# Squared-ReLU MLP of a decoder step: the down projection by Strassen's seven products, in a second pass over operands kept in DRAM

## The chip, the cores and the metric

The kernel runs on one core of one Trainium2 chip. The metric is the device time of one execution in microseconds (us); a lower time is better. The engines are TensorE (PE, its weight loads PEld), VectorE (DVE), ScalarE (ACT), GpSimd (POOL) and SyncE (SP), which issues DMAs. Each engine works through its own instructions in the order in which they were emitted, and waits on semaphores for the others.

## The reference

One layer of a decoder trunk on 1024 prompt tokens and 8 new tokens (T = 1032 columns) with 1024 features. Sparse attention and a gated mixing branch make `m`; the change is in what follows:

```python
    x = x + m @ w_o                                  # 1024 x 1024
    hf = rmsnorm(x, g_ffn)
    x = x + jnp.square(jax.nn.relu(hf @ w_up)) @ w_down   # 1024 -> 4096 -> 1024
    hp = rmsnorm(x, g_ple)
    x = x + jax.nn.sigmoid(hp @ w_pg) * (p @ w_p)    # p has 256 features
```

## The kernel before

Features lie on the 128 partitions and tokens along the free dimension. Every large product is made in float32 precision out of three matmuls: operand and weight are split into a rounded high part and the rest (`hh`, `hl`; `whi`, `wlo`), and `hi*hi`, `hi*lo`, `lo*hi` are added up in PSUM. A high part is an ACT cast, the rest a DVE or POOL subtraction behind it. `dense` makes such a product in three groups of 344 tokens, each in one of four PSUM banks of tag "mm"; `weight()` loads and splits blocks of 128x1024 weights (512 KB) ahead of their use.

The MLP runs over 8 blocks `f` of 512 hidden features. In each block, four column blocks of `w_up` (72 matmuls of 344 columns each) leave PSUM through DVE: `z = p * n1.R`, where `R` is the token's norm scale along the free dimension, then relu and square in one DVE operation, then the ACT cast `hh` and the POOL subtraction `hl`. Behind them, four blocks of `w_down` are multiplied with `hh`, `hl`, and DVE adds each PSUM group onto `x1`. So both projections are 2304 matmuls of 344 columns. In the last block the second norm follows each finished `x1[k]`: `split` is an ACT activation `nh` and a DVE operation `nl`; `square` is an ACT square and a POOL addition onto `acc` (the last one on DVE). The loop on the per-layer embedding then makes, for each of 8 column blocks, 18 matmuls of `p @ w_p` (leaving through ACT as `e`) and 72 of `w_pg`.

All of these tiles come out of one pool of 37 slots of 128x1032 floats (tag "s", reused first in, first out); a `wide` tile has all 8x1032 columns, and there is one. There is no scheduler at this place: the order of the emitted Python is the order on every engine.

Of the kernel before, what the change touches and what calls it, by code (L numbers as in the profile page):

```python
# [16 lines left out]
P = 128  # L17
# [16 lines left out]
FFB = 8  # L34
EPS = 1e-6
# [13 lines left out]
class Counted:  # L49
    """An engine whose instructions' estimated times are added up as they are emitted."""  # L50
# [15 lines left out]
def step_kernel(ctx, tc, xT, pT, w_in, w_o, w_up, w_down, w_pg, w_p, gv, gqk, wsT, b_s,  # L66
# [55 lines left out]
    # ------------------------------------------------------------ order of emission  # L122
# [46 lines left out]
    # ------------------------------------------------------------ weights, two blocks ahead  # L169
    plan = [(w_in[c], KC, pool if c > 1 else dve) for c in range(w_in.shape[0])]  # L170
    plan += [(w_o[c], KC, dve) for c in range(KC)]
    for f in range(FFB):
        plan += [(w_up[4 * f + c], KC, dve) for c in range(4)]
        plan += [(w_down[f, c], 8, dve) for c in range(4)]
    for c in range(KC):
        plan += [(w_p[c], 2, dve), (w_pg[c], KC, dve)]
# [19 lines left out]
    def weight():  # L196
        n = at[0]
        at[0] += 1
        split_weight(n)
        if n + 1 != w_in.shape[0]:  # L200
            split_weight(n + 1)
        if not n + 1 <= w_in.shape[0] <= n + 2:
            load_weight(n + 2)
        if n + 1 < len(plan) and plan[n + 1][1] < KC:
            split_weight(n + 2)
            load_weight(n + 3)
# [14 lines left out]
    def dense_in_step(A, jobs, hook=None, lag=0):  # L221
        """As dense for several blocks of weights (weights, groups, PSUM), block of features by block of
        features, for operands that are still being made."""
        n = len(A[0])
        for step in range(n + lag * (len(jobs) - 1)):
            for j, ((hi, lo), groups, outs) in enumerate(jobs):
                k = step - lag * j
                if not 0 <= k < n:
                    continue
                for w, x in ((hi, A[0]), (hi, A[1]), (lo, A[0])):  # L230
                    for (a, b), p in zip(groups, outs):
                        mm(p[:, :b - a], w[:, k, :], x[k][:, a:b],
                           start=(k == 0 and w is hi and x is A[0]), stop=(k == n - 1 and w is lo))
# [33 lines left out]
    def inv_rms(sq, n, name, then, make=bank2, wait=later):  # L267
        """sq [P, T]: squares, summed over blocks of features -> [token of tile, tile] of rsqrt(mean + eps)."""
# [11 lines left out]
    def along_tokens(r, name):  # L280
        """[token of tile, tile] -> the same values along the free dimension, on every partition."""
# [10 lines left out]
    def across(out, col):  # L292
        """A column of values along the free dimension of 64 partitions."""
# [3 lines left out]
    # ------------------------------------------------------------ constants, and the input's pre-norm  # L297
# [28 lines left out]
    # work for the tensor engine until the first operands arrive  # L326
# [40 lines left out]
    # ------------------------------------------------------------ indexer keys, weights and queries  # L367
# [9 lines left out]
    def split_heads(q, a, b, p, then=None):  # L377
        """Two heads' features -> for each its high part on its own 64 partitions, the low part on the others."""
# [65 lines left out]
    # ------------------------------------------------------------ scores and their top keys  # L444
# [76 lines left out]
    # ------------------------------------------------------------ queries and keys  # L521
# [5 lines left out]
    def head_scale(sq, f, then=None):  # L527
        """sq [P = two heads, T] -> f [token of tile, tile, head] = r / sqrt(r^2 mean + eps)."""
# [82 lines left out]
    # ------------------------------------------------------------ values  # L611
# [27 lines left out]
    # ------------------------------------------------------------ decode: 8 new tokens over paged keys  # L639
# [191 lines left out]
    # ------------------------------------------------------------ the attention branch's gate  # L831
# [9 lines left out]
    # ------------------------------------------------------------ the spatial gating branch  # L841
# [124 lines left out]
    # ------------------------------------------------------------ prompt attention  # L966
# [47 lines left out]
    # the rest of the last gate's projection fills the tensor engine while the attention starts  # L1014
# [179 lines left out]
    # the new tokens' rows, then the halves that the output projection starts with  # L1194
# [26 lines left out]
    # ------------------------------------------------------------ output projection  # L1221
# [5 lines left out]

    def in_step(A, hook=None, W=None):
        return dense_in_step(A, [(W or weight(), GROUPS, [bank("acc") for _ in GROUPS])], hook)[0]
# [172 lines left out]
```

## Time and the profile before

| | us |
|---|---|
| time, median of 3 runs (lowest to highest) | 1866.78 (1866.0 to 1867.72) |
| span of the profiled execution | 1864.2 |
| PE busy in the span | 1826.8 (98%) |
| DVE, ACT, POOL busy in the span | 1105.0, 605.4, 437.0 |

The span is that of one profiled execution, from its first to its last instruction; the time of a run also holds what lies around the span, some 2.6 us. Shares of busy time are means over stages that have different limits. In the trace, a matmul's row shows when it starts and how long it is in the pipeline; since matmuls overlap, what one costs in a stream is the distance from start to start.

### The profile page before, as it was taken

To read this page: it belongs to the slowest core of one execution; us is meant where nothing else is said; L and a number is where in the kernel's file an instruction comes from. 1 tells how busy PE (TensorE), PEld (TensorE's weight loads), DVE (VectorE), ACT (ScalarE), POOL (GpSimd) and SP (SyncE) were. 2 spreads that over 40 slices of the span, in tenths; PEclk is the share of its full clock that TensorE was granted. 3 is DMA by queue.
4 is the path that set the end of the run, shared out by engine and by line. 5 is a ranking of instruction groups with operands and counts; after the bars stand their busy time and mean duration, and the time that the engine had idled before them with its cause. 6 is when DMAs were issued, how large, how long until landed. Compare 5 with 4: busy or idle time off the path is not lost.

```text
span 1864.2 us, 28776 instructions
## 1 busy us (share of the span) xinstructions
PE 1826.8 (98%) x11722; PEld 1724.2 (92%) x11722; DVE 1105.0 (59%) x2110; ACT 605.4 (32%) x1084; POOL 437.0 (23%) x375
## 2 busy tenths in 40 slices
PE   8999989999999999999999999999999999999998
PEld 8998879998999996777699999999999999999998
DVE  7489978989877856777743434333333333335433
ACT  5554332244312136777622202020202020113322
POOL 3233354456323221110011202010101011112221
PEclk9999989999999999999999999999999999999999
DMA  4122133222222264223232111111111111111121
GB/s 171 61 93 102 58 111 105 86 86 96 64 91 77 83 165 118 60 64 94 68 117 69 34 57 45 47 46 46 46 46 46 46 46 55 48 46 49 43 77 72
DMA packets 81748, 136.66 MB, mean 73 GB/s; under 512 B 9608, under 2 KB 54544, under 8 KB 81616
## 3 DMA queue, kind: packets, MB, share of 16 engines
q1 hardware_dynamic: 79424, 130.08, 21.3%
q0 software_dynamic: 2048, 4.72, 0.8%
q8 instruction: 92, 1.51, 0.3%
q14 instruction: 40, 0.33, 0.1%
q10 hardware_dynamic: 144, 0.02, 0.0%
HBM read 105.03 MB, written 29.77 MB: 72 GB/s over the span
## 4 chain that ended last, share of the span: by engine, by line
PE 83%; DVE 7%; issue 3%; POOL 3%; ACT 1%; DMA 1%; SPq 0%; POOLq 0%; DVEq 0%; ACTq 0%
PE acc L60 69%; PE po L60 4%; PE sc L60 4%; PE pp L60 4%; DVE mask L60 3%; DVE m L60 1%; POOL wlo L193 1%; DVE qs L60 1%; PE mix L60 1%; DMA kib<-cache_ki,idx 1%; POOL pg L651 0%; PE lg L60 0%; PE dix L60 0%; PE vt L60 0%; POOL x L342 0%
## 5 line engine op out<-in xcount | busy, mean ns | idle before, releaser
L60 PE MATMUL acc<-xh,whi 128*128 128x344 f32 (+1 forms) x1144 | 373.1, 329 | 2.8 <-DVE s_q L60 1.8
L60 PE MATMUL acc<-xl,whi 128*128 128x344 f32 (+1 forms) x1144 | 365.3, 323 | 2.2 <-DVE xl L60 2.2
L60 PE MATMUL acc<-xh,wlo 128*128 128x344 f32 (+1 forms) x1144 | 365.3, 323 | 1.8 <-POOL r_x L270 1.1
L60 PE MATMUL acc<-nh,whi 128*128 128x344 f32 x960 | 302.6, 320 | 0.4 <-DVE y L60 0.3
L60 PE MATMUL acc<-nh,wlo 128*128 128x344 f32 x960 | 301.5, 319 | 0.0
L60 PE MATMUL acc<-nl,whi 128*128 128x344 f32 x960 | 301.4, 319 | 0.0
L60 PE MATMUL acc<-hh,whi 128*128 128x344 f32 x768 | 245.7, 320 | 0.0
L60 PE MATMUL acc<-hl,whi 128*128 128x344 f32 x768 | 245.5, 320 | 0.0
L60 PE MATMUL acc<-hh,wlo 128*128 128x344 f32 x768 | 245.3, 319 | 0.0
L60 DVE TENSOR_TENSOR x<-acc,x 128x344 f32<-128x344 f32 x216 | 109.3, 514 | 224.6 <-PE acc L60 224.6
L60 PEld LDWEIGHTS acc<-xh,whi 128*128 128x128 f32 x1144 | 216.6, 190 | 11.5 <-issue 5.0
L1290 POOL TENSOR_TENSOR hl<-z,hh 128x344 fp32r<-128x344 f32 x96 | 90.0, 938 | 584.8 <-ACT hh L1289 563.6
L60 PEld LDWEIGHTS acc<-xl,whi 128*128 128x128 f32 x1144 | 216.4, 190 | 3.6 <-DVE xl L60 3.2
L60 PEld LDWEIGHTS acc<-xh,wlo 128*128 128x128 f32 x1144 | 216.2, 190 | 2.7 <-POOL r_x L270 1.5
L1289 ACT CAST hh<-z 128x344 fp32r<-128x344 f32 x96 | 46.1, 480 | 501.0 <-DVE z L60 501.0
L60 PEld LDWEIGHTS acc<-nh,whi 128*128 128x128 f32 x960 | 179.3, 188 | 2.1 <-issue 0.8
L60 PEld LDWEIGHTS acc<-nh,wlo 128*128 128x128 f32 x960 | 179.4, 188 | 0.0
L60 PEld LDWEIGHTS acc<-nl,whi 128*128 128x128 f32 x960 | 179.4, 188 | 0.0
L60 DVE MATCH_REPLACE8 mask<-m,mask 128x384 f32<-128x384 f32 (+2 forms) x192 | 166.6, 875 | 0.0
L192 ACT CAST whi<-wraw 128x1024 fp32r<-128x1024 f32 (+1 forms) x136 | 134.4, 1006 | 91.8 <-DMA wraw<-w_up 66.0
L60 DVE TENSOR_TENSOR wlo<-wraw,whi 128x1024 fp32r<-128x1024 f32 (+1 forms) x91 | 108.9, 1198 | 92.9 <-ACT whi L192 88.8
L60 DVE MAX8 m<-mask 128x8 f32<-128x384 f32 (+2 forms) x192 | 161.0, 879 | 0.0
(266 smaller groups left out, 2901.4 us busy)
## 6 DMA issues: line engine op xcount, KB each, us to landing
wraw<-w_in SPq DMA_DIRECT2D x48, 512.0 KB, 3.7
wraw<-w_up SPq DMA_DIRECT2D x32, 512.0 KB, 3.1
wraw<-w_down SPq DMA_DIRECT2D x32, 512.0 KB, 3.1
q_d<-qs SPq DMA_DIRECT2D x16, 512.0 KB, 3.2
qst<-q_d SPq DMA_DIRECT2D x16, 512.0 KB, 4.9
x<-xT SPq DMA_DIRECT2D x15, 516.0 KB, 8.4
sga_d<-sg SPq DMA_DIRECT2D x8, 516.0 KB, 2.9
msgu_d<-u SPq DMA_DIRECT2D x8, 516.0 KB
```

The costliest lines, as they stand in the source:

```text
L60: return fn(*args, **kw)
L192: act.copy(hi, raws[n])
L193: eng.tensor_tensor(out=lo, in0=raws[n], in1=hi.bitcast(F32), op=ALU.subtract)
L1289: act.copy(h[:, a:b], z)
L1290: pool.tensor_tensor(out=l[:, a:b], in0=z, in1=h[:, a:b].bitcast(F32), op=ALU.subtract)
```

## The change

The hidden layer is no longer used as it is made. In a first pass over all 8 blocks, the up projection's PSUM groups leave through ACT (relu) and POOL (square), without the norm scale. With the hidden features of a block cut into two halves and the tokens into two halves of 516 (`TH`), a 2x2 block matrix is there, and `operands` makes the seven right-hand operands of Strassen's scheme (Winograd's form) of it: four are differences of 516 columns on DVE; each of the seven is split into a high part (ACT cast) and a rest (DVE subtraction) in a slot `hop`. They go to a DRAM scratch `h_d`, except those of the last block, which stay in SBUF and are the first of the second pass.

The second pass has 32 steps (8 blocks `f`, the resident block first, and 4 output pairs `o`). A step loads 512 KB of `w_down`, makes four sums of 256 columns on POOL, splits three weights and four sums (ACT casts, DVE subtractions `dlo`), and runs seven products `a`, `b`, `c`, `d` of 12 matmuls of 258 columns (`TQ`) each: 2688 in all. What a product gives is added by DVE onto `acc` and `u2` in SBUF (in the first block it is copied by ACT). In the last block, `u2` is added, the result is multiplied by `R2 = R*R`, the residual `xr` is loaded again from DRAM and added (POOL, for the last pair DVE), and the second norm follows. The embedding's products are made in two halves of 72 matmuls, one between the passes (`embed(0)`) and one behind the second (`embed(1)`), and go through a DRAM scratch `e_d`.

The core of the diff (lines are left out where `...` stands):

```diff
+    h_d = drm.tile([FFB - 1, 7, 2, P, 2, TH], F32, name="h_d")
+    e_d = drm.tile([P, KC, T], F32, name="e_d")
+    hw = wide("hw")
+    own_ops = {}
+    pieces = []
...
+        def keep(i, src):
+            def piece():
+                op = slot("hop", [P, 2, TH], F32R)
+                act.copy(op[:, 0], src)
+                dve.tensor_tensor(out=op[:, 1], in0=src, in1=op[:, 0].bitcast(F32), op=ALU.subtract)
+                if f == DOWN[0]:
+                    own_ops[i, j] = op
+                else:
+                    sp.dma_start(out=h_d[f, i, :, :, j, :].rearrange("h p t -> p h t"), in_=op.bitcast(F32))
+            return piece
+        return [keep(0, b11), less(t1, b12, b11), keep(1, t1), keep(2, b21), keep(3, b22), less(t3, b22, b12),
+                keep(4, t3), less(t2, b22, t1), keep(5, t2), less(t4, b21, t2), keep(6, t4)]
+    for f in range(FFB):
+        for j in range(2):
+            row = 4 * j
+            for q, c in enumerate((j, j + 2)):
+                h = hw[:, row + q, :]
+                for a, b, p in (dense(X1) if f + j + q else in_step(X1, n1.hook)):
+                    z = part("z")
+                    act.activation(z, p, AF.Relu)
+                    pool.tensor_tensor(out=h[:, a:b], in0=z, in1=z, op=ALU.mult)
+                    for _ in range(2):
+                        if pieces:
+                            pieces.pop(0)()
+            while pieces:
+                pieces.pop(0)()
+            pieces = operands(f, j, row)
+    R2 = n1.R
+    pool.tensor_tensor(out=R2, in0=R2, in1=R2, op=ALU.mult)
...
+    def embed(g, between=None):
+        ph, pl = [], []
+        for k in range(2):
+            e = slot("pe")
+            sp.dma_start(out=e, in_=pT[k])
+            h, l = slot("ph", dt=F32R), slot("pl", dt=F32R)
+            act.copy(h, e)
+            dve.tensor_tensor(out=l, in0=e, in1=h.bitcast(F32), op=ALU.subtract)
+            ph.append(h)
+            pl.append(l)
+        raw = slot("pwraw", [P, 4, 2, P])
+        hi, lo = slot("pwhi", [P, 4, 2, P], F32R), slot("pwlo", [P, 4, 2, P], F32R)
+        sp.dma_start(out=raw, in_=w_p[4 * g:4 * g + 4].rearrange("c p k m -> p c k m"))
+        act.copy(hi, raw)
+        dve.tensor_tensor(out=lo, in0=raw, in1=hi.bitcast(F32), op=ALU.subtract)
+        def project():
+            for n in range(4):
+                e = slot("e")
+                for a, b, p in dense((ph, pl), W=(hi[:, n], lo[:, n])):
+                    act.activation(e[:, a:b], p, AF.Copy, scale=0.5)
+                sp.dma_start(out=e_d[:, 4 * g + n, :], in_=e)
+        return project
...
+    steps = [(f, o) for f in DOWN for o in range(4)]
...
+    def down_sums(n):
+        if n < len(steps):
+            w = draw[n]
+            a11, a12, a22, a21 = (w[:, q] for q in range(4))
+            ds[n] = s_ = slot("ds", [P, 4, 2, P])
+            pool.tensor_tensor(out=s_[:, 0], in0=a21, in1=a22, op=ALU.add)
+            pool.tensor_tensor(out=s_[:, 1], in0=s_[:, 0], in1=a11, op=ALU.subtract)
+            pool.tensor_tensor(out=s_[:, 2], in0=a11, in1=a21, op=ALU.subtract)
+            pool.tensor_tensor(out=s_[:, 3], in0=a12, in1=s_[:, 1], op=ALU.subtract)
...
+        def to(self, out, first):
+            views = [(out.rearrange("p (s c) -> p s c", s=2), self.all)] if self.one else \
+                [(out[:, TQ * s:TQ * s + TQ], self.at[s]) for s in range(2)]
+            for o, p in views:
+                if first:
+                    act.copy(o, p)
+                else:
+                    dve.tensor_tensor(out=o, in0=p, in1=o, op=ALU.add)
...
+    def product(n, f, i, w, pair, start):
+        hi, lo = dhalf[n, w[0]]
+        hi, lo = hi[:, w[1]], lo[:, w[1]]
+        for j in range(2):
+            xh, xl = right(f, i, j)
+            for l, x in ((hi, xh), (hi, xl), (lo, xh)):
+                for s in range(2):
+                    mm(pair.at[s], l[:, j, :], x[:, TQ * s:TQ * s + TQ],
+                       start=(start and j == 0 and l is hi and x is xh),
+                       stop=(j == 1 and l is lo), skip_group_check=not start)
...
+    first_embed = embed(0)
+    down_sums(0)
+    for part_ in range(2):
+        down_hi(0, part_)
+        down_lo(0, part_)
+    first_embed()
+    while pieces:
+        pieces.pop(0)()
+    acc = wide("acc")
+    u2s = [slot("u2", [P, 2, TH]) for _ in range(2)]
-    for f in range(FFB):
...
+    for n, (f, o) in enumerate(steps):
+        down_load(n + 2)
+        first, last = f == DOWN[0], f == DOWN[-1]
...
         if last:
-            n2 = Norm(3, "2")
...
+            xr = [slot("xr") for _ in range(2)]
+            for h in range(2):
+                sp.dma_start(out=xr[h], in_=x1_d[:, o + 4 * h, :])
...
+        a = Pair("pa", True)
+        product(n, f, 0, A11, a, True)
+        a.to(u2, first)
+        d = Pair("pd", True)
+        product(n, f, 1, S1, d, True)
+        d.to(c22, first)
+        down_sums(n + 1)
+        down_hi(n + 1, 0)
+        product(n, f, 2, A12, a, False)
+        a.to(c11, first)
+        free(2)
+        product(n, f, 3, S4, d, False)
+        d.to(d12, first)
+        free(3)
+        down_lo(n + 1, 0)
+        down_hi(n + 1, 1)
+        c = Pair("pc", False)
+        product(n, f, 4, S3, c, True)
+        c.to(c22, False)
+        free(4)
+        b = Pair("pb", False)
+        product(n, f, 5, S2, b, True)
+        b.to(u2, False)
+        free(5)
+        down_lo(n + 1, 1)
+        product(n, f, 6, A22, c, False)
+        c.to(c21, first)
+        free(6)
...
+        if last:
+            dve.tensor_tensor(out=d12, in0=d12, in1=u2, op=ALU.add)
+            both = acc[:, 2 * o + 1, :].rearrange("p (s c) -> p s c", s=2)
+            dve.tensor_tensor(out=both, in0=both, in1=u2.unsqueeze(1).to_broadcast([P, 2, TH]), op=ALU.add)
+            for h in range(2):
+                k = o + 4 * h
+                x = n2.x[k]
+                dve.tensor_tensor(out=x, in0=x, in1=R2, op=ALU.mult)
+                (pool if o < 3 else dve).tensor_tensor(out=x, in0=x, in1=xr[h], op=ALU.add)
+                n2.square(k)
+            for k in ((), (0, 4), (1, 5), ())[o]:
+                n2.split(k)
+    last_embed = embed(1)
+    load_weight(at_pg)
+    load_weight(at_pg + 1)
+    for k in (2, 6, 3, 7):
+        n2.split(k)
+    split_weight(at_pg)
+    last_embed()
...
     for k in range(KC):
         e = slot("e")
-        for a, b, p in dense((ph, pl)):
-            act.activation(e[:, a:b], p, AF.Copy, scale=0.5)
+        sp.dma_start(out=e, in_=e_d[:, k, :])
```

On PE, one block of the down projection before the change is 24 matmuls of 344 columns for each token group, of which these are the first; `acc` is the PSUM bank:

```order
L60 MATMUL acc<-hh,whi 128x344
L60 MATMUL acc<-hl,whi 128x344
L60 MATMUL acc<-hh,wlo 128x344
L60 MATMUL acc<-hh,whi 128x344
```

After the change, one product of a step is these rows; both token quarters use one weight, so that two matmuls of 258 columns stand behind each other:

```order
L63 MATMUL pa<-hop,dhi 128x258 x4
L63 MATMUL pa<-hop,dlo 128x258 x2
L63 MATMUL pa<-hop,dhi 128x258 x4
L63 MATMUL pa<-hop,dlo 128x258 x2
```

On ACT, between the two passes of the changed kernel stand these rows (`ph`, `pwhi` belong to the embedding, `e` is its result, `hop` are operands of the resident block, `u_13652` is `u2`):

```order
L1338 CAST ph<-pe 128x1032 x2
L1345 CAST pwhi<-pwraw 128x1024
L1382 CAST dhi<-draw 128x768
L1382 CAST dhi<-ds 128x1024
L1352 ACTIVATE e<-acc 128x344 x12
L1301 CAST hop<-hw 128x516 x7
L1428 COPY u_13652<-pa 128x516
L1428 COPY acc<-pd 128x516
```

The seven casts of the resident block's second half now stand behind the embedding's twelve copies, and ahead of the copies that free the first two products' PSUM.

On DVE, from the end of the second last-block step (`o = 1`) to the third's first additions, the changed kernel has these rows:

```order
L63 TENSOR_TENSOR acc<-pc,acc 128x258 x2
L63 TENSOR_TENSOR acc<-acc,u_13652 128x516
L63 TENSOR_TENSOR acc<-acc,u_13652 128x1032
L63 TENSOR_TENSOR acc<-acc,R_10208 128x1032 x2
L63 SCALAR_TENSOR_TENSOR nl<-acc,gvt,nh 128x1032 x2
L63 TENSOR_TENSOR u_13653<-pa,u_13653 128x516
L63 TENSOR_TENSOR acc<-pd,acc 128x516
```

Before the change, the last block's rows on DVE are additions out of PSUM with one `nl` after every third:

```order
L60 TENSOR_TENSOR x_9369<-acc,x_9369 128x344 x3
L60 SCALAR_TENSOR_TENSOR nl<-x_9369,gvt,nh 128x1032
L60 TENSOR_TENSOR wlo<-wraw,whi 128x1024
L60 TENSOR_TENSOR x_9369<-acc,x_9369 128x344 x3
```

So the addition `u_13653<-pa`, which frees a product's PSUM, now stands behind two `nl`, and these behind the ACT and POOL rows of the same place:

```order
L1247 ACTIVATE sq<-acc 128x1032 x2
L240 ACTIVATE nh<-acc,gvt 128x1032 x2
L1382 CAST dhi<-draw 128x768
```

```order
L1521 TENSOR_TENSOR acc<-acc,xr 128x1032
L1249 TENSOR_TENSOR acc<-acc,sq 128x1032
L1521 TENSOR_TENSOR acc<-acc,xr 128x1032
L1249 TENSOR_TENSOR acc<-acc,sq 128x1032
L1372 TENSOR_TENSOR ds<-draw 128x256
```

The first fence is ACT's and the second POOL's: each square waits for POOL's residual addition, and POOL's second residual addition stands behind its addition of the first square.

## Rows read from the trace of the kernel before

**Rows 1.** The page: span, and busy time, share and instructions of each engine.

```profile
span 1864.2 us, 28776 instructions
...
PE 1826.8 (98%) x11722; PEld 1724.2 (92%) x11722; DVE 1105.0 (59%) x2110; ACT 605.4 (32%) x1084; POOL 437.0 (23%) x375
```

**Rows 2.** Windows of MLP and second norm: engines' busy us, clock, DMA share, GB/s.

```profile
1019.00:1730.00 711.00, 711.00 (x4524) 710.53 (x4517) 277.48 (x449) 119.57 (x173) 101.02 (x101) 1.00 0.14 47
1730.00:1763.00 33.00, 31.93 (x201) 29.60 (x200) 15.68 (x23) 12.86 (x20) 9.65 (x7) 1.00 0.07 24
```

**Rows 3.** Chain that ended last: start, us, engine, group.

```profile
503.03 1.78 PE mix L60 x16
...
1026.48 703.15 PE acc L60 x4464
```

**Rows 4.** PE in order of time: start, us in the pipeline.

```profile
152.62 0.39 PE L60 MATMUL lg<-kih,qis 128*128 128x512 f32 x1
152.85 0.39 PE L60 MATMUL lg<-kil,qis 128*128 128x512 f32 x1
153.09 0.28 PE L60 MATMUL lg<-kih,qis 128*128 128x256 f32 x1
153.21 0.28 PE L60 MATMUL lg<-kil,qis 128*128 128x256 f32 x1
153.32 0.33 PE L60 MATMUL acc<-xh,whi 128*128 128x344 f32 x1
```

**Rows 5.** Groups from 922 us on, shapes apart: busy us, mean ns, idle before.

```profile
L60 PE MATMUL acc<-hh,whi 128*128 128x344 f32 x768 | 245.7, 320 | 0.0
...
L60 DVE TENSOR_TENSOR x<-acc,x 128x344 f32<-128x344 f32 x216 | 109.3, 514 | 224.6 <-PE acc L60 224.6
...
L1290 POOL TENSOR_TENSOR hl<-z,hh 128x344 fp32r<-128x344 f32 x96 | 90.0, 938 | 584.8 <-ACT hh L1289 563.6 <-issue 21.2
L192 ACT CAST whi<-wraw 128x1024 fp32r<-128x1024 f32 x79 | 80.4, 1044 | 91.8 <-DMA wraw<-w_up 66.0 <-DMA wraw<-w_pg 25.8
...
L1317 ACT ACTIVATE e<-acc 128x344 f32<-128x344 f32 x24 | 10.3, 453 | 4.9 <-PE acc L60 4.9
...
L1185 POOL TENSOR_TENSOR m<-g,ms 128x256 f32<-128x256 f32 x1 | 0.7, 729 | 2.3 <-DVE g L60 2.3
```

**Rows 6.** DVE in order of time; in brackets the idle time before.

```profile
947.75 2.51 DVE L60 SCALAR_TENSOR_TENSOR nl<-x,gvt,nh 128x1032 fp32r<-128x1032 f32 x1 [2.18 <-ACT nh L240]
950.18 1.21 DVE L60 TENSOR_TENSOR wlo<-wraw,whi 128x1024 fp32r<-128x1024 f32 x1
```

**Rows 7.** POOL at the same place.

```profile
946.74 2.42 POOL L1246 TENSOR_TENSOR acc<-acc,sq 128x1032 f32<-128x1032 f32 x1 [23.31 <-ACT sq L1244]
```

**Rows 8.** DVE while POOL is idle.

```profile
1742.90 1.29 DVE L60 SCALAR_TENSOR_TENSOR nl<-x,gvt,nh 128x1032 fp32r<-128x1032 f32 x1 [1.29 <-ACT nh L240]
```

**Rows 9.** DVE and ACT at the end of the down projection.

```profile
1728.50 0.93 DVE L60 TENSOR_TENSOR x<-acc,x 128x344 f32<-128x344 f32 x2
...
1731.53 1.29 DVE L60 SCALAR_TENSOR_TENSOR nl<-x,gvt,nh 128x1032 fp32r<-128x1032 f32 x1 [1.36 <-ACT nh L240]
...
1730.27 1.16 ACT L240 ACTIVATE nh<-x,gvt 128x1032 fp32r<-128x1032 f32 x1 [2.05 <-DVE x L60]
```

**Rows 10.** POOL at that place.

```profile
1728.36 2.51 POOL L1246 TENSOR_TENSOR acc<-acc,sq 128x1032 f32<-128x1032 f32 x1 [4.71 <-ACT sq L1244]
```

**Rows 11.** The last matmul of the kernel, and DVE's first operation behind it.

```profile
1858.68 0.32 PE L60 MATMUL acc<-nh,wlo 128*128 128x344 f32 x1
...
1859.04 0.52 DVE L60 TENSOR_TENSOR y<-acc,R 128x344 f32<-128x344 f32 x1 [1.63 <-PE acc L60]
```

**Rows 12.** PE behind a long idle time in the attention part.

```profile
252.62 0.76 PE L60 MATMUL lg<-kih,qis 128*128 128x512 f32 x1 [5.00 <-ACT rl L469]
```

**Rows 13.** Windows around it: columns as in Rows 2.

```profile
246.00:252.60 6.60, 1.62 (x11) 1.33 (x9) 5.08 (x8) 1.47 (x3) 6.43 (x3) 1.00 0.48 179
252.70:256.00 3.30, 3.30 (x12) 2.81 (x13) 3.30 (x5) 2.49 (x4) 2.08 (x3) 0.50 0.06 20
```

**Rows 14.** The window with the most DMA.

```profile
4.00:12.00 8.00, 6.78 (x26) 5.45 (x26) 4.71 (x7) 5.19 (x8) 1.91 (x1) 1.00 0.98 354
```

More of the change, by code (lines that the diff above doesn't have):

```diff
@@ L34 @@
 FFB = 8
+TH = T // 2
+TQ = T // 4
+DOWN = [FFB - 1] + list(range(FFB - 1))
 EPS = 1e-6
@@ L171, in step_kernel @@
     plan += [(w_o[c], KC, dve) for c in range(KC)]
-    for f in range(FFB):
[L173 to L176, printed above, removed]
+    plan += [(w_up[4 * f + c], KC, dve) for f in range(FFB) for c in (0, 2, 1, 3)]
+    at_pg = len(plan)
+    plan += [(w_pg[c], KC, dve) for c in range(KC)]
+    pauses = (w_in.shape[0], at_pg)
     raws, halves = {}, {}
@@ L1263, in step_kernel @@
     M = (mh, ml)
-    n1 = Norm(2, "1")
+    n1 = Norm(2, "1", x1)
     for k in range(KC):
@@ new lines, in step_kernel, with down_load @@
+    steps = [(f, o) for f in DOWN for o in range(4)]
+    draw, dhalf, ds = {}, {}, {}
+    def down_load(n):
+        if n < len(steps):
+            f, o = steps[n]
+            draw[n] = slot("draw", [P, 4, 2, P])
+            sp.dma_start(out=draw[n], in_=w_down[f, o])
+    def down_sums(n):
+        if n < len(steps):
+            w = draw[n]
[5 more added lines that the diff above has]
+            pool.tensor_tensor(out=s_[:, 3], in0=a12, in1=s_[:, 1], op=ALU.subtract)
@@ new lines, in down_hi, with down_lo @@
+    def down_hi(n, part_):
+        if n < len(steps):
+            src = ds[n] if part_ else draw[n][:, :3]
+            k = 4 if part_ else 3
+            hi = slot("dhi", [P, k, 2, P], F32R)
+            act.copy(hi, src)
+            dhalf[n, part_] = [hi, None]
+    def down_lo(n, part_):
+        if n < len(steps):
+            src = ds.pop(n) if part_ else draw[n][:, :3]
+            k = 4 if part_ else 3
+            hi = dhalf[n, part_][0]
+            lo = slot("dlo", [P, k, 2, P], F32R)
+            dve.tensor_tensor(out=lo, in0=src, in1=hi.bitcast(F32), op=ALU.subtract)
+            dhalf[n, part_][1] = lo
@@ new lines, in step_kernel, with load_op, right, __init__ @@
+    ops = {DOWN[0]: own_ops}
+    def load_op(f, i):
+        if f is None:
+            return
+        hl = [slot("hop", [P, 2, TH], F32R) for _ in range(2)]
+        for h in range(2):
+            sp.dma_start(out=hl[h].bitcast(F32), in_=h_d[f, i, h])
+        d = ops.setdefault(f, {})
+        for j in range(2):
+            d[i, j] = (hl[0][:, j], hl[1][:, j])
+    def right(f, i, j):
+        op = ops[f][i, j]
+        return op if isinstance(op, tuple) else (op[:, 0], op[:, 1])
+    class Pair:
+        def __init__(self, name, one):
+            self.one = one
+            if one:
+                t = bank2(name)
+                self.at = [t[:, 512 * s:512 * s + TQ] for s in range(2)]
+                self.all = t.rearrange("p (s c) -> p s c", s=2)[:, :, :TQ]
+            else:
+                self.at = [bank(name)[:, :TQ] for _ in range(2)]
+        def to(self, out, first):
[4 more added lines that the diff above has]
+                    act.copy(o, p)
+                else:
+                    dve.tensor_tensor(out=o, in0=p, in1=o, op=ALU.add)
@@ new lines, in step_kernel, with free @@
+    A11, A12, A22 = (0, 0), (0, 1), (0, 2)
+    S1, S2, S3, S4 = (1, 0), (1, 1), (1, 2), (1, 3)
+    down_load(0)
+    down_load(1)
+    first_embed = embed(0)
[8 more added lines that the diff above has]
+    u2s = [slot("u2", [P, 2, TH]) for _ in range(2)]
+    n2 = None
+    for n, (f, o) in enumerate(steps):
+        down_load(n + 2)
+        first, last = f == DOWN[0], f == DOWN[-1]
+        follows = None if last else DOWN[DOWN.index(f) + 1]
+        c11, d12 = acc[:, 2 * o, :TH], acc[:, 2 * o, TH:]
+        c21, c22 = acc[:, 2 * o + 1, :TH], acc[:, 2 * o + 1, TH:]
+        u2 = u2s[o // 2][:, o % 2]
+        if o == 1:
+            for i in range(2):
+                load_op(follows, i)
+        if last and o == 0:
+            n2 = Norm(3, "2", [acc[:, 2 * (k % 4) + k // 4, :] for k in range(KC)])
+        if last:
+            xr = [slot("xr") for _ in range(2)]
+            for h in range(2):
+                sp.dma_start(out=xr[h], in_=x1_d[:, o + 4 * h, :])
+        def free(i):
+            if o == 3 and i > 1:
+                load_op(follows, i)
+        a = Pair("pa", True)
[26 more added lines that the diff above has]
+        free(6)
+        dhalf.pop((n, 0))
+        dhalf.pop((n, 1))
+        draw.pop(n)
+        if o == 3:
+            ops.pop(f)
+        if last:
+            dve.tensor_tensor(out=d12, in0=d12, in1=u2, op=ALU.add)
+            both = acc[:, 2 * o + 1, :].rearrange("p (s c) -> p s c", s=2)
+            dve.tensor_tensor(out=both, in0=both, in1=u2.unsqueeze(1).to_broadcast([P, 2, TH]), op=ALU.add)
+            for h in range(2):
+                k = o + 4 * h
[5 more added lines that the diff above has]
+                n2.split(k)
```

89 lines of the change are left out of this document (35 added, 54 removed).

## Prediction

> **What bounds the kernel now.** I read the page first: PE is busy in 98% of the span, DVE in 59% [rows 1]. Then windows over the stages that change: from 1019 to 1730 us (w_up and w_down) PE is busy in all 711 us at full granted clock, DVE in 277, ACT in 120, POOL in 101, and DMA has a share of 0.14 [rows 2]. The chain that ended last runs through the same stretch as one uninterrupted piece of PE, 4464 matmuls in 703.15 us [rows 3]. So the MLP is a stream of matmuls without a gap, each of 344 columns and worth 703.15 / 4464 = 157.5 ns. Around the second norm PE idles only 33.00 - 31.93 = 1.07 us [rows 2]. A change here can only gain by fewer or cheaper matmuls, and everything that interrupts the stream costs its full length.
>
> **The gain.** The up projection keeps its 2304 matmuls of 344 columns, the embedding its 144, w_pg its 576. The down projection loses 2304 x 157.5 ns = 362.9 us (768 of each of three kinds [rows 5]) and gets 2688 matmuls of 258 columns. No row has 258. In a stream the starts lie 111 ns apart at 128 columns (1.78 us / 16 [rows 3]), 0.11 to 0.12 us at 256, 0.23 at 512 [rows 4]. A line through 344 and 512 gives 120 at 258, proportion to 344's price 118.1; I take 119: 319.9 us. **-43.0 us**, with ends at -45 and -40.
>
> The Trainium skill, "TensorE: Matmul & The Clock Gate", section "Back-to-back issue gap", speaks against this: it gives some 81 ns at 128 columns and 131 at 512 for sustained streams, so nearly a price by count. An estimate from that page, interpolated: 2304 x 109 = 251 us removed, 2688 x 98 = 263 added, +12 instead of -43. This trace's prices disagree with it.
>
> **Prices for the stalls**, all from rows. DVE: 344 columns out of PSUM 514 ns [rows 5], 1024 in 1.21 us [rows 6], so by a line 0.69 at 516, 0.42 at 258, 0.95 at 768, 1.22 at 1032; 0.08 less when one follows another (two in 0.93 [rows 9]). ACT: 453 ns at 344, 1044 at 1024 [rows 5], so 0.62 at 516, 0.83 at 768; nh 1.16 [rows 9]. POOL: 729 ns at 256, 938 at 344 [rows 5], 2.42 at 1032 [rows 7]. A hand-off between engines takes 0.1 us (nh ends at 1731.43, nl starts at 1731.53 [rows 9]), from PE's end of stream to DVE about 0.2 (1858.68 + 0.16, then 1859.04 [rows 11]).
>
> One more price is hidden in the rows: nl at 947.75 took 2.51 us while POOL added from 946.74 to 949.16, and 1.29 us where POOL was idle [rows 6 to 8]. So a DVE operation with both inputs in SBUF waits for a POOL addition in progress. Additions out of PSUM don't (two in 0.93 us inside a POOL addition [rows 9, 10]). I call this the exclusion, and give each stall with and without it.
>
> **Stalls between the passes.** (a) From the last up matmul to the embedding: ACT makes relu, a hop cast, ph twice and pwhi, done at 4.2 us; POOL's last square and R*R (2.42 us) keep DVE's subtraction waiting, then DVE works off its remainder, pl, pl and pwlo, which the embedding's third matmul needs. **+8.1** (5.6 without exclusion, 9.6 if DVE and POOL take turns). (b) The embedding's 72 matmuls hide nothing of the last operands, because the seven hop casts stand behind its twelve copies on ACT. ACT and DVE then hand on to each other (casts 0.62, eleven DVE operations of 0.61 to 0.69); the last cast ends 10.8 us after the embedding's last matmul, and only then ACT copies u2, ready at 11.4. The third product reuses that PSUM pair, and could start at 24 x 0.119 = 2.86. **+8.5.**
>
> **28 ordinary steps.** A step lasts 84 x 0.119 = 10.0 us. DVE has four additions of 516 columns, six of 258 and two dlo (0.95, 1.21), 6.4 us in a row to 7.5 with waits for POOL's four sums (0.73 each); each addition has a product's time (1.43 us) to free its PSUM and needs 0.2 + 0.7 to 0.9. Margins are some 0.3 us: **0**, but 0.4 us a step, +11 in all, where the exclusion falls badly. Scratch DMA: per block 7.4 MB of operands and 2.1 of w_down in 40 us, 237 GB/s, against 354 at a share of 0.98 [rows 14]; loads are issued 10 us ahead or more: 0. In pass one ACT, DVE and POOL have less or similar work per group than now, under PE's 3.8 us: 0.
>
> **The last block.** Here DVE, ACT and POOL pass each finished x around, and the next step's first addition (u2<-pa, which frees PSUM for its third product) stands behind it on DVE. Counted from the end of the seventh product of step 30 (third of the four): additions out of pc end at 1.3, u2 onto d12 at 1.9, onto both at 3.1, R2 at 4.3 and 5.45; POOL adds the residual to 7.85; ACT squares to 9.0; POOL adds the square to 11.55 and the second residual to 13.95; ACT squares to 15.1, then nh to 16.15; DVE's nl waits for it, and for POOL's next addition (to 17.65): 18.9, 20.1; u2<-pa 20.75. The third product starts at 20.85 instead of 2.86: **+18.0** (15.6 without exclusion). The same walk at the other places:
> - first step's end: DVE's five operations alone (5.45), then u2<-pa: **+3.3**;
> - inside the second step: dhi behind the squares, dlo behind POOL, and only then the addition that frees pc: **+3.4** (1.75);
> - third step's second product, whose sums, dhi and dlo come late: **+1.65**;
> - second step's end, as worked out for the third, POOL with one more addition ahead: **+19.3** (16.5);
> - fourth step's end: DVE now adds the residuals too (7.7), squares, ph, ph, pwhi on ACT, DVE's addition of the last square behind POOL, pl, pl, pwlo: **+14.6** (13.5). The remaining four nl then lie under the embedding's 11.3 us.
>
> Together **+60.2** (52.3 without exclusion).
>
> **Clock.** After PE had idled 5.00 us [rows 12], the granted clock in the next 3.3 us was 0.50, that is 1.2 GHz for 2.4, while it was 1.00 before [rows 13]: 3.3 us of matmuls did half the work, 1.7 us lost. Five stalls here idle PE 6 us or more: **+8.5**, between 0 and 17.
>
> **Sum.** -43.0 + 8.1 + 8.5 + 60.2 + 8.5 = **+42.3**. The profiled execution's 1864.2 us of span becomes 1906.5; with the same 2.6 us around it (1866.78 is the median) the time is **1909 us**. Its own range, from ends of -45 to -40, of the clock and of (a), is 1900 to 1920.
>
> **Rivals.**
> - *Norm and additions don't queue* (the other side): the two chains at the ends of the second and third step and the exclusion cost nothing, because POOL and ACT are through when DVE's queue gets there. Then only the other places stall: -43 + 8.1 + 8.5 + 8.35 + 14.6 and 5 for the clock = +1.5, and without exclusion and clock loss -8.7: **1858 to 1868**. It decides as soon as all stalls with the clock sum to less than 43 us. For it speaks that before the change nl stands between additions without stopping PE (DVE waits 1.36 us there [rows 9]); against it, that each next product needs the very addition queued behind nl.
> - *No exclusion*: stalls of 5.6 + 8.5 + 52.3 = 66.4, with the clock's 8.5 and -43.0: +31.9, **1898.6**. For it speaks that the slowed rows could be a busy moment of DVE; against it, that their length fits POOL's end.
> - *DVE saturates ordinary steps*: 0.4 to 1 us in each of 28, +11 to +28: **1920 to 1937**. For it speak margins of 0.3 us; against, DVE's 75% at most.
> - *Pass two is bound by DMA*: were only 200 GB/s to be had for scratch, each of seven blocks would take 9.5 MB / 200 = 47.5 us for 40: +52, **1961**. For it speaks that the scratch is read and written in pieces of a few KB; the 354 GB/s [rows 14] speak against it.
> - *Narrower matmuls hardly get cheaper*: on a line from 111 ns at 128 columns to 157.5 at 344, 258 costs 139, and 2688 of them 374 us: +11 instead of -43, **1963**. The starts at 256 columns [rows 4] speak against it, but they are few, and among wider ones.
>
> The Trainium skill's section on the issue gap, named above, is a rule of that last kind; the time by its figures is an estimated 1964.
>
> **How the numbers follow.** My forecast 0.56; no exclusion 0.20; saturated steps 0.11; no queueing 0.07; DMA 0.03; dear narrow matmuls 0.03. The range that leaves out some 2 in 10, since cases mix, is **1886 to 1936**: it holds the forecast, no exclusion with a smaller clock loss, and most of the saturated steps. A measurement here tells 0.2% (3.7 us) from no change. Faster by more has only the no-queueing case's lower part and unseen savings: 0.06; within it 0.02; slower 0.92.
>
> **What would show it.** In the changed profile's chain of waits, PE should be interrupted at some seven places by DVE (u2, c, pwlo) and ACT (u2 copy); matmuls of 258 columns should lie 119 ns apart, 7 x 12 x 0.119 = 10.0 us per step; PE's idle before the first additions of the third and fourth last-block steps some 18 us each; behind each such gap a clock of 0.5. Wrong it would be if windows of ordinary steps show PE idle (saturation, DMA), if the 258-column distance isn't 119, or if nl lies at 1.3 us with POOL busy.

## The result

The changed kernel takes 1910.21 us in the median (1907.4 to 1911.23, four runs), the kernel before, measured with it, 1866.71 (1866.0 to 1867.72): a ratio of 1.0232, 95% interval 1.0217 to 1.0246, so it is slower by 43.5 us. The profiled execution has a span 45.0 us longer than that of before, of which 0.4 us lie ahead of the changed part. The page of the changed kernel begins:

```profile
span 1909.2 us, 30609 instructions
...
PE 1803.7 (94%) x12106; PEld 1698.9 (89%) x12106; DVE 1234.7 (65%) x2244; ACT 702.8 (37%) x1248; POOL 557.0 (29%) x510
```

PE is busy for 23 us less than before [rows 1], with 384 more matmuls, and idles for 68 us more. Windows show where (the columns are those of [rows 2]): the first pass, the place between the passes in two pieces, most of the 28 ordinary steps of the second pass, and the last block with the second norm.

```profile
1027.00:1378.60 351.60, 351.60 (x2232) 351.31 (x2232) 154.87 (x194) 125.86 (x231) 72.31 (x95) 1.00 0.55 196
1378.60:1399.00 20.40, 13.29 (x71) 12.69 (x72) 9.82 (x6) 10.43 (x18) 13.23 (x10) 0.83 0.19 75
1399.00:1412.00 13.00, 4.54 (x29) 3.70 (x28) 8.61 (x11) 5.12 (x10) 4.06 (x4) 0.80 0.79 292
1412.00:1690.00 278.00, 278.00 (x2292) 278.00 (x2292) 176.15 (x303) 63.16 (x79) 90.82 (x104) 0.99 0.61 222
1690.00:1800.00 110.00, 57.20 (x386) 54.87 (x386) 65.68 (x84) 26.44 (x27) 44.33 (x25) 0.73 0.25 90
```

The first pass and the ordinary steps have no idle PE, at a DMA share of 0.55 and 0.61 and with DVE busy for 63% of the steps. The idle time that was added stands in the three windows left: 7.11, 8.46 and 52.80 us, 68.4 together, in places where the granted clock is also lower.

PE in order of time gives each place; the bracket is the idle time and what ended it:

```profile
1382.56 0.42 PE L63 MATMUL acc<-ph,pwhi 128*128 128x344 f32 x1 [3.96 <-ACT pwhi L1345]
1383.45 0.65 PE L63 MATMUL acc<-pl,pwhi 128*128 128x344 f32 x1 [0.46 <-DVE pl L63]
1386.79 0.66 PE L63 MATMUL acc<-ph,pwlo 128*128 128x344 f32 x1 [2.68 <-DVE pwlo L63]
...
1411.60 0.80 PE L63 MATMUL pa<-hop,dhi 128*128 128x258 f32 x2 [7.68 <-ACT u L1428]
...
1674.16 0.65 PE L63 MATMUL pa<-hop,dhi 128*128 128x258 f32 x4
...
1684.29 0.64 PE L63 MATMUL pa<-hop,dhi 128*128 128x258 f32 x4
...
1710.40 1.09 PE L63 MATMUL pa<-hop,dhi 128*128 128x258 f32 x4 [2.82 <-DVE u L63]
...
1719.16 0.96 PE L63 MATMUL pc<-hop,dhi 128*128 128x258 f32 x4 [1.21 <-DVE acc L63]
...
1722.69 0.76 PE L63 MATMUL pd<-hop,dhi 128*128 128x258 f32 x4 [0.17 <-ACT dhi L1382]
1723.95 0.51 PE L63 MATMUL pd<-hop,dlo 128*128 128x258 f32 x2 [0.50 <-DVE dlo L63]
...
1743.62 0.58 PE L63 MATMUL pa<-hop,dhi 128*128 128x258 f32 x1 [18.45 <-DVE u L63]
...
1772.71 0.58 PE L63 MATMUL pa<-hop,dhi 128*128 128x258 f32 x1 [16.72 <-DVE u L63]
...
1794.21 0.66 PE L63 MATMUL acc<-ph,pwhi 128*128 128x344 f32 x1 [11.30 <-ACT pwhi L1345]
...
1797.13 0.65 PE L63 MATMUL acc<-ph,pwlo 128*128 128x344 f32 x1 [1.62 <-DVE pwlo L63]
```

Two rows without a bracket are the starts of two ordinary steps: 1684.29 - 1674.16 = 10.13 us, 120.6 ns for each of 84 matmuls. The down projection's 2688 matmuls cost 324.2 us, 38.7 less than the 362.9 that they replace. Idle time took 68.4 - 1.07 = 67.3 back. What is left of the 44.6 us, 44.6 + 38.7 - 67.3 = 16.0, is matmuls at less than full speed behind the gaps, and PE's new start after each. The first part can be read from the starts: the stretches that begin at 1386.79, 1411.60, 1710.40, 1743.62, 1772.71 and 1797.13 last 1.4, 2.5, 1.6, 2.1, 2.8 and 2.6 us longer than their matmuls take at 157.5 or 120.6 ns, together 13.0 us.

How the two longest of these waits come about is read on the three engines at the second of them (16.72 us, behind the third of the last four steps), DVE first, then ACT, then POOL:

```profile
1755.79 2.37 DVE L63 TENSOR_TENSOR acc<-acc,R 128x1032 f32<-128x1032 f32 x2
1768.39 3.66 DVE L63 SCALAR_TENSOR_TENSOR nl<-acc,gvt,nh 128x1032 fp32r<-128x1032 f32 x2 [10.23 <-ACT nh L240]
1771.98 0.68 DVE L63 TENSOR_TENSOR u<-pa,u 128x516 f32<-128x516 f32 x1
...
1766.25 1.06 ACT L1247 ACTIVATE sq<-acc 128x1032 f32<-128x1032 f32 x1 [4.78 <-POOL acc L1521]
1767.22 2.19 ACT L240 ACTIVATE nh<-acc,gvt 128x1032 fp32r<-128x1032 f32 x2
...
1757.10 3.28 POOL L1521 TENSOR_TENSOR acc<-acc,xr 128x1032 f32<-128x1032 f32 x1 [12.15 <-DVE acc L63]
1761.55 2.36 POOL L1249 TENSOR_TENSOR acc<-acc,sq 128x1032 f32<-128x1032 f32 x1 [1.17 <-ACT sq L1247]
1763.86 2.36 POOL L1521 TENSOR_TENSOR acc<-acc,xr 128x1032 f32<-128x1032 f32 x1
1767.39 2.37 POOL L1249 TENSOR_TENSOR acc<-acc,sq 128x1032 f32<-128x1032 f32 x1 [1.17 <-ACT sq L1247]
```

DVE is through with R2 at 1758.16 and waits 10.23 us for nh, because the addition that PE needs is third in its queue. Nh stands behind a square, the square behind POOL's second residual addition, and that behind POOL's addition of the first square. Then two nl take 3.66 us and not 2.45, since POOL adds from 1767.39 to 1769.76.

The clock behind the gaps at 1411.60, 1743.62 and 1772.71, in windows:

```profile
1411.60:1417.10 5.50, 5.50 (x25) 5.50 (x26) 1.15 (x2) 1.91 (x3) 0.00 (x0) 0.51 0.29 95
...
1743.70:1747.30 3.60, 3.60 (x17) 3.60 (x18) 1.16 (x2) 1.04 (x1) 1.24 (x2) 0.50 0.00 0
...
1772.70:1778.70 6.00, 5.99 (x28) 5.99 (x29) 1.68 (x3) 0.00 (x0) 0.00 (x0) 0.50 0.29 90
```

In the second, 17 matmuls take 3.60 us at a granted clock of 0.50 (1.2 GHz for 2.4), where 30 fit in at 120.6 ns; in the first, 25 take 5.50 us, and in the third, 28 take 6.00.

### The profile page after: what moved, and what is told of

The parts are those of the page before. It is cut to its first block, busy times and chain, and to the rows that moved or that the text cites. A ratio compares the mean times of both kernels' runs of the same rounds, so it can differ in the third digit from the quotient of the medians.

```text
span 1909.2 us, 30609 instructions
## 1 busy us (share of the span) xinstructions
PE 1803.7 (94%) x12106; PEld 1698.9 (89%) x12106; DVE 1234.7 (65%) x2244; ACT 702.8 (37%) x1248; POOL 557.0 (29%) x510
## 4 chain that ended last, share of the span: by engine, by line
PE 79%; DVE 9%; POOL 4%; issue 4%; ACT 2%; DMA 2%; another core or an unknown queue 0%; SPq 0%; POOLq 0%; DVEq 0%; ACTq 0%
PE acc L63 49%; PE pa L63 5%; PE pd L63 4%; PE pc L63 4%; PE po L63 4%; PE pp L63 3%; PE sc L63 3%; DVE mask L63 3%; PE pb L63 2%; DVE m L63 2%; POOL wlo L195 1%; POOL acc L1521 1%; PE mix L63 1%; DMA kib<-cache_ki,idx 1%; PE lg L63 1%
## 5 line engine op out<-in xcount | busy, mean ns | idle before, releaser
L63 DVE TENSOR_TENSOR hop<-hw,hop 128x516 fp32r<-128x516 f32 x112 | 88.5, 802 | 197.0 <-ACT hop L1301 163.6
L195 POOL TENSOR_TENSOR wlo<-wraw,whi 128x1024 fp32r<-128x1024 f32 x47 | 113.5, 2416 | 159.1 <-ACT whi L194 98.1
L1320 POOL TENSOR_TENSOR hw<-z 128x344 f32<-128x344 f32 x96 | 73.1, 762 | 283.0 <-ACT z L1319 283.0
L63 PE MATMUL pa<-hop,dhi 128*128 128x258 f32 x512 | 86.7, 293 | 46.2 <-DVE u L63 38.0
L1319 ACT ACTIVATE z<-acc 128x344 f32<-128x344 f32 x96 | 43.8, 459 | 225.8 <-PE acc L63 225.8
L1112 ACT ACTIVATE p<-p,mx,s_q 128x1024 f32<-128x1024 f32 (+7 forms) x128 | 110.4, 865 | 22.6 <-DVE mx L63 21.9
L63 PEld LDWEIGHTS pa<-hop,dhi 128*128 128x128 f32 x512 | 73.7, 198 | 47.5 <-DVE u L63 38.6
L194 ACT CAST whi<-wraw 128x1024 fp32r<-128x1024 f32 x96 | 100.2, 1043 | 1.4 <-DMA wraw<-w_up 1.4
```

Source lines behind the costliest of these rows:

```text
L63: return fn(*args, **kw)
L194: act.copy(hi, raws[n])
L195: eng.tensor_tensor(out=lo, in0=raws[n], in1=hi.bitcast(F32), op=ALU.subtract)
L1112: eng.activation(s, s, AF.Exp, bias=env["mx"][:, 4 + h:5 + h], scale=sc, accum_out=env["sum"][:, h:h + 1])
L1319: act.activation(z, p, AF.Relu)
L1320: pool.tensor_tensor(out=h[:, a:b], in0=z, in1=z, op=ALU.mult)
```

## The experiments

The theory to test is that of the prediction: the products gain some 40 us, and order alone loses it, since at each place an operation on which PE waits is queued behind operations on which it doesn't. Rivals are that a limit of the engines themselves (POOL's chain, DVE's total) holds the time, that DMA makes matmuls dearer, and that the low clock has another cause than idleness. Each run was timed against the kernel before on the same chip (medians of before 1865.27 to 1866.18), so ratios are to be compared first; what a run gains over the changed kernel (1.0232) is given by them.

**Splits ahead of squares.** In the last block:

```diff
                 (pool if o < 3 else dve).tensor_tensor(out=x, in0=x, in1=xr[h], op=ALU.add)
-                n2.square(k)
             for k in ((), (0, 4), (1, 5), ())[o]:
                 n2.split(k)
+            for h in range(2):
+                n2.square(o + 4 * h)
```

> One line of order in the last block: the second norm's splits (nh on ACT, nl on DVE) are emitted ahead of the two squares of the same step, not behind them. Theory (the queues): nl, and behind it u2<-pa, wait only because ACT's nh stands behind squares that wait for two POOL additions; the two long gaps, 18.6 and 16.9 us in the changed kernel, fall to 6 to 9 us each (c.to, d12, both, R2 twice, nl twice, with a POOL addition in the way), and the time to 1887 to 1895. Rival (POOL's chain of four additions is itself the limit, wherever the splits stand): the gaps stay within 2 us and the time within 5 us of 1910.

1893.69 us, ratio 1.0153 (1.0136 to 1.0170). The time is in the theory's range, 15 us below the changed kernel, and the rival falls. But the two long gaps fell to 10.37 and 9.71 us only, not to 6 to 9:

```profile
1708.38 0.75 PE L63 MATMUL pa<-hop,dhi 128*128 128x258 f32 x4 [2.82 <-DVE u L63]
...
1717.15 1.29 PE L63 MATMUL pc<-hop,dhi 128*128 128x258 f32 x4 [2.74 <-DVE acc L63]
...
1733.83 1.23 PE L63 MATMUL pa<-hop,dhi 128*128 128x258 f32 x4 [10.37 <-DVE u L63]
...
1755.79 1.23 PE L63 MATMUL pa<-hop,dhi 128*128 128x258 f32 x4 [9.71 <-DVE u L63]
```

The rest is in DVE's and POOL's rows of this kernel:

```profile
1726.48 6.69 DVE L63 SCALAR_TENSOR_TENSOR nl<-acc,gvt,nh 128x1032 fp32r<-128x1032 f32 x2
...
1725.50 6.58 POOL L1521 TENSOR_TENSOR acc<-acc,xr 128x1032 f32<-128x1032 f32 x2 [5.97 <-DVE acc L63]
```

Nothing is late any more for nl, yet two of them take 6.69 us for 2.45, while two POOL additions take 6.58 for 4.84. Each engine's operations are held up while the other's run; that I had counted once, and it happened at each.

The first two of PE's rows above hold something else. The wait of 2.82 us is the changed kernel's at 1710.40, but here the clock behind it stayed up:

```profile
1708.40:1714.00 5.60, 5.60 (x46) 5.60 (x47) 1.92 (x3) 2.66 (x3) 4.42 (x3) 1.00 0.00 0
```

So PE was sooner at the seventh product, which goes into `pc`, and waited 2.74 us there, where the changed kernel, with 1.6 us lost to the clock, waited 1.21.

**The place between the passes.** The embedding's casts go ahead of the last up block, the resident operands and the first step's weight splits (`split_down`) between the embedding's copies, R*R behind them:

```diff
+                if f == FFB - 1 and j + q == 2:
+                    first_embed = embed(0)
...
-    first_embed()
-    while pieces:
-        pieces.pop(0)()
+    first_embed(pieces[:2] + [lambda: split_down(0)] + pieces[2:5] + [lambda: split_down(1)] + pieces[5:10])
+    for piece in pieces[10:]:
+        piece()
+    R2 = n1.R
+    pool.tensor_tensor(out=R2, in0=R2, in1=R2, op=ALU.mult)
```

> Only the place between the passes: the embedding's casts and subtractions are emitted one column block earlier, R*R behind the embedding, and the resident block's last operands one by one between the embedding's copies. Theory: the gaps of 8.0 us (a) and 9.1 us (b) fall to under 1.5 us each, with some 4 us of low clock behind them: 1910 to 1888 to 1894. Rival (the 37 slots or the exclusion between DVE and POOL move the wait into the embedding): less than 8 us gained.

1893.52 us, ratio 1.0149 (1.0132 to 1.0166), within the theory's range and 15 us below the changed kernel. The first gap is gone; the second is smaller, but not under 1.5 us. PE's row, and ACT's two before it:

```profile
1396.34 1.23 PE L63 MATMUL pa<-hop,dhi 128*128 128x258 f32 x4 [4.04 <-ACT u L1430]
...
1395.18 0.62 ACT L1301 CAST hop<-hw 128x516 fp32r<-128x516 f32 x1 [1.01 <-DVE hw L63]
1395.71 0.58 ACT L1430 COPY u<-pa 128x516 f32<-128x516 f32 x1
```

The copy of u2 is still behind the last hop cast, and that cast waits for a difference on DVE: casts and differences hand on to one another also when they lie under the embedding.

**No reload of operands.**

```diff
     def load_op(f, i):
-        if f is None:
-            return
+        return
...
-        op = ops[f][i, j]
+        op = own_ops[i, j]
```

> All blocks of the second pass use the resident block's operands; the 98 loads of 516 KB from the scratch are left out, so the result is not the reference's. Theory (no product waits for a transfer, and 120.6 ns is the price of a 258-column matmul): within 2 us of 1910, matmul distance unchanged. Rival (DMA traffic into SBUF makes the operand reads dearer, 120.6 in place of 119): 4 us less, with the distance at 119 or below in the ordinary steps.

1908.44 us, ratio 1.0230 (1.0213 to 1.0247; the changed kernel's 1.0232 lies in it). DMA's share in the steps falls from 0.61 to 0.16, PE's rows hardly change:

```profile
1412.00:1690.00 278.00, 278.00 (x2291) 278.00 (x2290) 175.11 (x304) 64.86 (x81) 79.99 (x105) 0.99 0.16 54
```

```profile
1674.29 0.64 PE L63 MATMUL pa<-hop,dhi 128*128 128x258 f32 x4
...
1684.38 0.64 PE L63 MATMUL pa<-hop,dhi 128*128 128x258 f32 x4
```

A step takes 10.09 us for 10.13. Over 28 steps that is some 1 us: the reads back from DRAM cost about nothing, and 120 ns is the matmul's price without them.

**Residual by DVE.**

```diff
-                (pool if o < 3 else dve).tensor_tensor(out=x, in0=x, in1=xr[h], op=ALU.add)
+                dve.tensor_tensor(out=x, in0=x, in1=xr[h], op=ALU.add)
```

> In the last block the residual is added by DVE in all four steps, not by POOL in the first three. Theory (two POOL additions of 2.4 to 3.3 us are on the path of the long gaps, a DVE addition is 1.2): gaps at the ends of the second and third step 10 to 12 us for 18.6 and 16.9, the gap behind the first step 5 to 6 for 3.0, the one inside the second step 0: 1895 to 1900. Rival (DVE's queue is the limit): the time stays or grows, since DVE gets 7 us of work more.

1896.24 us, ratio 1.0168 (1.0151 to 1.0185), within the theory's range. The gaps behind the first three of the last four steps:

```profile
1712.61 1.23 PE L63 MATMUL pa<-hop,dhi 128*128 128x258 f32 x4 [5.35 <-DVE u L63]
...
1736.70 1.23 PE L63 MATMUL pa<-hop,dhi 128*128 128x258 f32 x4 [12.21 <-DVE u L63]
...
1760.74 1.23 PE L63 MATMUL pa<-hop,dhi 128*128 128x258 f32 x4 [12.19 <-DVE u L63]
```

This is as worked out for the chain through POOL, with the two long ones just above their 10 to 12 us: the first grows, the other two shrink, the small one inside the second step is gone. DVE has more work and the kernel is faster.

**Keeping PE at work.**

```diff
+        c = Pair("pc", False)
+        if last and o > 1:
+            for _ in range(130):
+                mm(c.at[0], dhalf[n, 0][0][:, 0, 0, :], right(f, 0, 0)[0][:, :TQ], start=True, stop=True)
         product(n, f, 2, A12, a, False)
```

> As the changed kernel, with 130 needless matmuls of 258 columns (15.7 us) between the second and the third product of the last block's third and fourth step, where PE waits 18.6 and 16.9 us; their result is overwritten. Theory (after a long wait of PE the granted clock is at half for some us of matmuls: 2.1 and 2.8 us lost behind these two waits): the waits' ends stay where they are, no half-speed matmuls behind them, 4 to 5 us less than the changed kernel. Rival (the low clock is the chip's at this time of the kernel, whatever PE does, or the loss is only the first matmuls' start): no change, within 1.5 us.

1907.12 us, ratio 1.0222 (1.0205 to 1.0239): 2 us below the changed kernel, not the 4 to 5 expected, and the intervals overlap, so the time alone doesn't decide. The rows are:

```profile
1743.46 1.23 PE L63 MATMUL pa<-hop,dhi 128*128 128x258 f32 x4 [2.73 <-DVE u L63]
...
1772.15 0.75 PE L63 MATMUL pa<-hop,dhi 128*128 128x258 f32 x4 [1.33 <-DVE u L63]
```

```profile
1743.60:1747.20 3.60, 3.60 (x19) 3.60 (x20) 1.11 (x2) 1.04 (x1) 1.17 (x2) 0.59 0.00 0
1772.20:1775.80 3.60, 3.60 (x30) 3.60 (x31) 1.66 (x3) 0.00 (x0) 0.00 (x0) 1.00 0.31 86
```

The waits' ends stayed (1743.46 and 1772.15 for 1743.62 and 1772.71). Behind the second wait, where 1.33 us of idleness were left, 30 matmuls run in 3.60 us at a clock of 1.00, 17 in the changed kernel; behind the first, with 2.73 us left, it is still 19 at 0.59, so that half of the expectation was missed. At the second place the rival falls: the place in the kernel is the same, PE's work before it is not, and the low clock is gone. The first place decides nothing, since idle times of this length went both ways: the 2.82 us ahead of 1710.40 were followed by half clock in the changed kernel, those in the first run above were not.

**All places at once.** If the work around the products is the loss, the same products with that work elsewhere should beat the kernel before. This is more than order: R*R and the last block's multiplications by R2 are gone, and the residual's additions take the place of ACT's copies. Beside the place between the passes as above: the norm scale goes on the way up, the residual is added with the first block's results, and a step's end is done one step later.

```diff
-                    act.activation(z, p, AF.Relu)
+                    dve.scalar_tensor_tensor(out=z, in0=p, scalar=0.0, in1=n1.R[:, a:b], op0=ALU.max, op1=ALU.mult)
...
-        d.to(c22, first)
+        d.to(c22, first, r22)
+        if last:
+            finish_u(o - 1, 0)
...
-        a.to(c11, first)
+        a.to(c11, first, r11)
+        if last:
+            finish_u(o - 1, 1)
...
         down_hi(n + 1, 1)
+        if last and o:
+            n2.square(o - 1)
+            n2.square(o + 3)
+        if last and o == 0:
+            last_embed = embed(1)
...
+    last_embed([lambda: split_weight(at_pg), lambda: n2.split_lo(5), lambda: n2.square(7), lambda: hi_lo(2),
+                lambda: hi_lo(6), lambda: hi_lo(3), lambda: hi_lo(7)])
```

Here `r11` to `r22` are views of the residual, `finish_u` adds u2 to a step's results, and `split_lo`, `hi_lo` are the two halves of a split.

> The seven products as they are, and all work around them moved: norm scale by DVE on the way up (max and multiply in one operation out of PSUM, in place of ACT's relu), residual added with the first block's results (DVE, in place of ACT's copies), so that the last block only adds u2, one step later, behind the next step's first additions; squares and nh spread over the steps, nl and the rest under the embedding's second half, whose casts are made a step earlier; the place between the passes as in the kernel e2_seam. Theory (the loss is the queues at seven places and the clock behind them, the products themselves gain 362.9 - 324 = 39 us): before's time - 39 + 4 (between the passes) + 2 to 8 elsewhere: 1830 to 1842, faster than the kernel before. Rival (the second pass has a cost of its own that the seams hide, for instance DVE's queue, now with 9 to 10 us of work per step in the last block, or 50 us more on it in pass one): 1850 or more.

1842.38 us, ratio 0.9876 (0.9860 to 0.9893): faster than the kernel before by 24 us, 0.4 us above the theory's range and well below the rival's. Four waits were left, the last of 1.06 us; the others are:

```profile
1395.35 1.23 PE L63 MATMUL pa<-hop,dhi 128*128 128x258 f32 x4 [2.89 <-ACT u L1443]
1400.39 1.23 PE L63 MATMUL pd<-hop,dhi 128*128 128x258 f32 x4 [2.09 <-DVE acc L63]
...
1694.15 0.96 PE L63 MATMUL pc<-hop,dhi 128*128 128x258 f32 x4 [3.58 <-DVE acc L63]
```

**The remaining waits.** In the same manner:

```diff
-        return [keep(0, b11), less(t1, b12, b11), keep(1, t1), keep(2, b21), keep(3, b22), less(t3, b22, b12),
-                keep(4, t3), less(t2, b22, t1), keep(5, t2), less(t4, b21, t2), keep(6, t4)]
+        return [less(t1, b12, b11), keep(0, b11), less(t2, b22, t1), keep(1, t1), less(t4, b21, t2), keep(2, b21),
+                keep(3, b22), less(t3, b22, b12), keep(4, t3), keep(5, t2), keep(6, t4)]
...
+        if last and o == 0:
+            parts.pop(0)()
```

`parts` holds the three preparations of the embedding's second half, which now stand at three places; the residual's first loads also stand ahead of the embedding's stores on SP.

> As e4_all_places, with its four remaining waits (3.06, 2.39, 3.74 and 1.22 us of PE, and 5 us of half clock behind them) taken up: the four differences of a block's operands come first, so that the casts no longer hand on to each other; the residual's first loads stand ahead of the embedding's stores on SP; the embedding's second preparation is spread over three places of the last block. Theory (each wait is the queue that the trace names): 8 to 13 us below e4's 1842.4, that is 1829 to 1835. Rival (DVE is full in pass two and the waits only move to the next operation): within 4 us of 1842.

1832.94 us, ratio 0.9822 (0.9809 to 0.9836), 33 us faster than the kernel before, 9 better than the one above, and within the theory's range. The waits left are 1.50, 1.11, 1.04 and 1.30 us. PE's idle time from the place between the passes to the second norm is down to a little over 5 us:

```profile
1377.00:1395.00 18.00, 16.50 (x112) 16.29 (x110) 15.15 (x17) 11.53 (x25) 11.18 (x10) 1.00 0.27 108
1395.00:1690.00 295.00, 293.89 (x2438) 293.69 (x2439) 201.10 (x349) 59.36 (x65) 103.77 (x116) 1.00 0.66 247
1690.00:1735.00 45.00, 42.31 (x312) 40.74 (x312) 40.16 (x51) 25.58 (x33) 21.64 (x11) 1.00 0.17 63
```

The clock is at 1.00 throughout, at the same places of the kernel where it was low before, and of the products' 38.7 us 33 have come out. What order alone gives back is shown by the first two runs, 15 us each; how the rest divides between order and the work taken elsewhere, no run separates.

## Why the prediction was right

It came out within 1.2 us of the median, but not each term did; the errors partly cancel, and that the sum is so close is partly luck. The forecast counted by how much the start of a matmul is late, which is up to 1 us more than PE's idle time; both are given below.

- **The products**: forecast -43.0, measured -38.7, outside its own ends of -45 and -40. The price of a matmul was the term mis-sized: 119 ns in the forecast, 120.6 in the trace, just above the line's end of 120. By the Trainium skill, "TensorE: Matmul & The Clock Gate", section "Back-to-back issue gap", it would be an estimated 98; this trace disagrees with that at 258 columns as it did at the other widths. The rivals of dear matmuls and of DMA fell with the ordinary steps' rows and with the run without reload.
- **Between the passes**: forecast 8.1 and 8.5. The starts are 8.0 us late at (a) and 9.5 at (b); the idle time at (a) is 7.10 (3.96, 0.46 and 2.68), at (b) 8.46. The queues named are those of the rows: pwhi, pl, pwlo, and the copy of u2.
- **Ordinary steps**: forecast 0, measured 0 in 278 us. The rival of a saturated DVE fell.
- **The last block**: forecast 3.3, 3.4, 1.65, 19.3, 18.0 and 14.6, together 60.2; the starts are 3.0, 1.4, 1.1, 18.6, 16.9 and 14.1 us late, together some 55, and PE's idle time in the window is 52.8. The walk through the third step holds row by row: counted from the end of the seventh product (1752.93), R2 is through at 5.2 us (forecast 5.45), POOL's first residual at 7.5 (7.85), ACT's second square at 14.4 (15.1), u2<-pa at 19.7 (20.75). Most mis-sized was the small wait inside the second step, 1.21 us idle for 3.4: the walk let PE run at full speed up to it, while behind the gap at 1710.40 its matmuls ran at half (1.09 us for a group of four that takes 0.64), so PE came 1.6 us later and waited less. In the first experiment, where the clock stayed up at this place, the wait was 2.74. Why the next one was 0.67 for 1.65 stays open.
- **The clock**: forecast 8.5 within 0 to 17, with five gaps of 1.7 each; measured 13.0 behind six gaps, of which the 1.6 behind 1710.40 only shortened the next wait. Two things were too small in that term: the gap of 2.82 us at 1710.40, not counted, lowered the clock too (though the same wait in the first experiment did not), and behind a long gap the low clock lasted up to 6.0 us of matmuls, not the 3.3 read in [rows 13]. That idleness is the cause, the run with needless matmuls showed at the one of its two places where little idleness was left, and the last run, without long gaps, bears it out.
- **The exclusion**: shown in the rows of nl (3.66 us for two, in the first experiment 6.69, for 2.45). The rival without it gave 1898.6, outside the measured runs, but the time would not have told: with 13.0 for the clock and -38.7 for the products its sum is 66.4 + 13.0 - 38.7 = 40.7, hence some 1907.5. That it works both ways, and lengthens POOL's additions too, was not in the sum.

Two smaller slips: the ends named for the products, the clock and (a) add up to 1896 to 1922, not 1900 to 1920; and what lies around the span is 1.7 us in each run of the changed kernel, since the 2.6 are a median less the span of one execution.

The rival on the other side (the norm's operations don't queue) was wrong for the changed kernel. The last two experiments bring about by order, and by work taken elsewhere, what it assumed; they end below its 1858, since the other stalls that it kept are gone too.

## What to carry to other kernels

Where one engine is busy without a gap, fewer operations for it pay only if nothing else is queued in front of what it waits for; list, for each place where stages meet, what stands ahead of the operation that frees its buffer. Work that is not needed soon (a norm's splits, the next stage's casts) belongs behind that operation, or a step later. And a cost that can be spread over a long stage with room (a scale on the way up, a residual at the first addition) should not wait for the end, where there is no cover.

## What was not expected of the hardware

- When both work on SBUF alone, DVE and POOL hold up each other; the forecast had only DVE waiting. Two nl took 6.69 us for 2.45, and two POOL additions at the same time 6.58 for 4.84.
- The same wait of PE, 2.82 us ahead of the third product of the second last-block step, was followed by a granted clock of 0.54 in the changed kernel (1710.40 to 1714.10) and of 1.00 in the first experiment; what decided between the two, no run here shows. Behind waits of 1.33 us (needless matmuls) and of 1.04 to 1.50 us (last run) the clock stayed at 1.00; behind a long wait the half clock lasted up to 6.0 us of work.
